# Weights of v in contiguous blocks, two loads cut in halves, and a new order for the first casts and products of an encoder layer

## The chip, the cores and the metric

The kernel runs on one core of one Trainium2 chip. The core has five engines that run their own instruction streams side by side: TensorE (PE, matrix products and transposes), VectorE (DVE), ScalarE (ACT), GpSimd (POOL) and SyncE (SP, which here only issues DMAs). TensorE reads SBUF and writes PSUM; DVE and ACT read PSUM, POOL does not. DMAs move data between HBM and SBUF. The metric is the device time of one execution in microseconds; smaller is better. Results are compared as the median of several runs.

## The reference

One layer of a bidirectional encoder on 1024 tokens of width 1024, in float32. The parts that matter here are the first ones: a LayerNorm of the input, and the products of its result with the columns of `w_in` that make q and v.

```python
def layer_norm(x, g, b):
    mu = jnp.mean(x, axis=-1, keepdims=True)
    var = jnp.mean(jnp.square(x - mu), axis=-1, keepdims=True)
    return (x - mu) * lax.rsqrt(var + LN_EPS) * g + b

h = layer_norm(x, emb_ln_g, emb_ln_b)                  # 1024 x 1024
proj = h @ w_in                                        # 1024 x 5120
q, k, v, z_a, u, z_b, g_a, g_b = jnp.split(proj, offs, axis=-1)
attn = neighbourhood_attention(q, k, v, rpb)           # 8 heads of 64
y_a = attn * silu(z_a)
h_lru = rg_lru(conv(u), forward) + rg_lru(conv(u), backward)
y_b = h_lru * silu(z_b)
m = sigmoid(g_a + b_merge[0]) * (y_a @ w_ba) + sigmoid(g_b + b_merge[1]) * (y_b @ w_bb)
out = layer_norm(ALPHA * h + m @ w_out, ln_g, ln_b)
```

## The kernel before

Tokens are handled in eight tiles of 128 (`x0` to `x7`), the width in eight blocks `k` of 128. Every float32 product is made of three products in a rounded format: an operand is split into a high part (a cast on ACT, names ending in `_hi`) and a low part (the difference between the value and its high part, names ending in `_lo`, on DVE or POOL). With activations `h` and weights `w` the three products are high times high, low times high and high times low. In `v_part(i, kind, ks)` (line 320) they are called `"h"` (high of h, high of w), `"a"` (low of h, high of w) and `"w"` (high of h, low of w); a tile of v takes 24 of them, eight blocks by three kinds, all added up in one PSUM bank.

The order of work is written out by hand for all engines: an engine runs its instructions in the order in which the program text issues them, and an instruction waits until its operands are there. An instruction that waits holds up everything behind it on its engine. On PE the order of the text is the order of the products. SP issues almost all loads and stores, in the order of the text too.

The stage that the change touches is the beginning, up to the first products of q, and it goes like this:

- Loads (lines 399 to 410): gains and biases of the LayerNorm, `x0` in two halves of 512 columns, v's weights in four loads of two blocks each (`load_wv`, line 191), `x1` between the second and the third, then `x2`, the first block of q's weights (`qk_load(0)`), `x3`, `x4` and some small tables. v's weights stand in HBM as 128 rows of 8 x 512 values, so that one load takes 4 KB out of each row of 16 KB.
- `warm_up(n)` (line 200) issues n small products of zeros on PE whose result is not used.
- `gb_spread` spreads the LayerNorm's gains and biases over all partitions, into four PSUM banks `gps`; `gb_copy(z, c)` (line 213, ACT) copies one of them to SBUF, where POOL can read it.
- The LayerNorm of a tile: `ln_stats` (DVE), `ln_root` (ACT), and then for tiles 0, 1 and 3 `ln_v(i, c)` (line 240, DVE, from the banks `gps`, one call per half of the columns), for the other tiles `ln_scale` (line 248, ACT) and `ln_g` (line 255, four operations on POOL, which need the copies of `gb_copy`; the first two make the left half, the last two the right one).
- `turn(i, kk)` (line 266): four transposes on PE of half a tile into one PSUM bank; `turn_hi` (line 278, ACT) and `turn_lo` (line 281, DVE) split the result into the blocks that the products read.
- `wv_hi(k)` (line 194, ACT) and `wv_lo(k)` (line 197, POOL) split block k of v's weights. `qk_prep(m)` (line 177) does the same for a block m of q's weights: `qk_hi` on ACT (line 171) and `qk_lo` on POOL. Only one raw block of q's weights fits at a time, so `qk_load(1)` can be issued when `qk_lo(0)` has read the first.
- `keep(i)` (line 261) stores a finished tile to HBM. `load_x(5)` goes into the place of `x0` and waits until `keep(0)` has landed.
- PE's own order in this stage: transposes of tile 0, 20 of the 24 products of v's tile 0, transposes of tile 1 with the rest of tile 0 and the products of tile 1 between them, 24 products of q (`q_part(0, 0)`, line 345, its matrix instructions stand in line 134), then 16 transposes: left half of tile 2, left half of tile 3, right half of tile 2, right half of tile 3 (`turned_in`, lines 512 to 518), then the products of v's tile 2.

PSUM banks of this stage come from a pool of four, in an order that the list `places` (line 86) writes out.

Of the kernel before, what the change touches and what calls it, by code (L numbers as in the profile page):

```python
# [15 lines left out]
P = 128  # L16
S = 1024
D = 1024
NK = D // P
# [4 lines left out]
HALF = 512  # L24
# [7 lines left out]
WARM = 18, 4, 6  # L32
# [35 lines left out]
def encoder_kernel(ctx, tc, x, gb1, gb, w_qk, w_v, w_s, w_ba, w_bb, w_gate, smalls, bias, w_out, out):  # L68
    nc = tc.nc
    V, A, G, PE, SP = nc.vector, nc.scalar, nc.gpsimd, nc.tensor, nc.sync  # L70
# [12 lines left out]
    hb12 = pool("hb12", "right")  # L83

    turns = []
    places = itertools.chain((0, 1, 2, 3, 0, 1, 2, 0, 2, 3, 1), itertools.cycle((2, 3, 0, 1)))

    def bank(name):
        if turns:
            return banks[0].tile([P, HALF], F32, tag=next(turns[0]), bufs=2, name=name)  # L90
        if banks[0] is ps0:
            return ps0.tile([P, HALF], F32, tag=f"b{next(places)}", bufs=1, name=name)
        return banks[0].tile([P, HALF], F32, tag="bank", name=name)
# [33 lines left out]
    def lo_of(eng, lo, full, hi):  # L127
        eng.tensor_tensor(lo, full, hi.bitcast(F32), ALU.subtract)  # L128
# [27 lines left out]
    wvs = [hts[0].tile([P, 4, HALF], F32, tag="ht4" + c, name=f"wvs{c}") for c in "hl"]  # L156
# [12 lines left out]
    def qk_hi(m):  # L169
        qk_w[m] = pair(wpl, [P, NK, P], f"wqk{m}", tag="w", bufs=2)  # L170
        A.copy(qk_w[m][0][:], qk_s[m][:])

    def qk_lo(m):
        hi, lo = qk_w[m]
        lo_of(G, lo[:], qk_s.pop(m)[:], hi[:])

    def qk_prep(m):
        qk_hi(m)
        qk_lo(m)
# [2 lines left out]

    def load_x(i):
        xs[i] = ln.tile([P, D], F32, tag="x", bufs=5, name=f"x{i}")
        if i == 0:
            for sl in halves:
                SP.dma_start(xs[i][:, sl], x[i][:, sl])
        else:
            SP.dma_start(xs[i][:], x[i])

    def load_wv(c):
        SP.dma_start(wvs[c // 2][:, 2 * (c % 2):2 * (c % 2) + 2, :], w_v[:, 2 * c:2 * c + 2, :])

    def wv_hi(k):
        A.copy(wv[0][k][:], wvs[k // 4][:, k % 4, :])

    def wv_lo(k):
        lo_of(G, wv[1][k][:], wvs[k // 4][:, k % 4, :], wv[0][k][:])

    def warm_up(n):  # L200
        for _ in range(n):
            PE.matmul(clock[:, :P], zero[:], zero[:], start=True, stop=True)
# [10 lines left out]
    def gb_copy(z, c):  # L213
        A.copy(gb_t[z][c][:], gps[z][c][:])

    def ln_stats(i):
        st, mv, e = (ln.tile([P, n], F32, tag=f"ln{n}{c}", bufs=2, name=f"ln{i}{c}")
                     for n, c in ((12, "t"), (2, "m"), (4, "e")))
        sts[i] = st, mv, e[:, 3:4], e[:, 0:3]
        sd, ve = sts[i][2:]  # L220
        for c in range(2):
            V.bn_stats(st[:, 6 * c:6 * c + 6], xs[i][:, halves[c]])
        V.bn_aggr(mv[:], st[:].rearrange("p (c s) -> p c s", c=2))
        V.tensor_scalar(ve[:, 0:1], mv[:, 1:2], EPS, -0.5, ALU.add, ALU.mult)

    def ln_root(i):
        st, mv, sd, ve = sts[i]
        A.activation(sd, mv[:, 1:2], AF.Sqrt, bias=eps_t[:])

    def ln_sums(i):  # L230
        ln_stats(i)
        ln_root(i)

    def ln_rstd(i):
        st, mv, sd, ve = sts[i]
        V.reciprocal(sd, sd)
        V.tensor_scalar(ve[:, 1:2], sd, sd, ve[:, 0:1], ALU.mult, ALU.mult)
        V.tensor_scalar(sd, ve[:, 1:2], 1.5, sd, ALU.add, ALU.mult)

    def ln_v(i, c):  # L240

        z, (st, mv, sd, ve), sl = xs[i], sts[i], halves[c]
        V.scalar_tensor_tensor(z[:, sl], z[:, sl], mv[:, 0:1], gps[0][c][:], ALU.subtract, ALU.mult)
        if c == 0:
            ln_rstd(i)
        V.scalar_tensor_tensor(z[:, sl], z[:, sl], sd, gps[1][c][:], ALU.mult, ALU.add)

    def ln_scale(i):

        z, (st, mv, sd, ve) = xs[i], sts[i]  # L250
        ln_rstd(i)
        V.tensor_scalar(ve[:, 2:3], mv[:, 0:1], -1.0, sd, ALU.mult, ALU.mult)
        A.activation(z[:], z[:], AF.Identity, bias=ve[:, 2:3], scale=sd)

    def ln_g(i):
        z = xs[i]
        for c in range(2):
            for w, op in enumerate((ALU.mult, ALU.add)):
                G.tensor_tensor(z[:, halves[c]], z[:, halves[c]], gb_t[w][c][:], op)
# [6 lines left out]
    def turn(i, kk):  # L266
        tp = tps[i, kk] = bank(f"tp{i}_{kk}")
        for k4 in range(4):
            k = 4 * kk + k4
            PE.transpose(tp[:, k4 * P:(k4 + 1) * P], xs[i][:, k * P:(k + 1) * P], ident[:])  # L270

    def ti(i):
        return slice((i % 4) * P, (i % 4 + 1) * P)

    def tp4(i, kk):
        return tps[i, kk][:].rearrange("p (k t) -> p k t", k=4)

    def turn_hi(i, kk):
        A.copy(blocks[kk][i // 4][0][:, :, ti(i)], tp4(i, kk))  # L279

    def turn_lo(i, kk):
        hi, lo = blocks[kk][i // 4]
        lo_of(V, lo[:, :, ti(i)], tp4(i, kk), hi[:, :, ti(i)])
# [36 lines left out]
    def v_part(i, kind, ks):  # L320

        if i not in vos:
            vos[i], vn[i] = bank(f"v{i}"), 0
        for k in ks:
            a = blocks[k // 4][i // 4][kind == "a"][:, k % 4, ti(i)]
            PE.matmul(vos[i][:], a, wv[kind == "w"][k][:], start=vn[i] == 0, stop=vn[i] == 23)  # L326
            vn[i] += 1
# [3 lines left out]
    def v_hi(i):  # L331
        vs = outs["v", i] = ln.tile([P, H, 2, DH], F32R, tag="vs", bufs=2, name=f"vs{i}")
        A.copy(vs[:, :, 0, :], vos[i][:].rearrange("p (h d) -> p h d", d=DH))
# [63 lines left out]
    K0, K1, KS, BOTH = range(4), range(4, 8), range(8), range(2)  # L397

    A.dma_start(gb_row[:], gb1.rearrange("o z (r f) -> (o z r) f", f=P))
    load_x(0)  # L400
    load_wv(0)
    load_wv(1)
    load_x(1)
    load_wv(2)
    load_wv(3)
    load_x(2)
    qk_load(0)
    load_x(3)
# [8 lines left out]
        gb_spread(z, c)  # L417
    warm_up(WARM[2])
    ln_sums(0)
    ln_v(0, 0)  # L420
    turn(0, 0)
    warm_up(WARM[2])
    wv_hi(0)
    wv_hi(1)
    turn_hi(0, 0)
    ln_v(0, 1)
    keep(0)
    load_x(5)
    turn(0, 1)
    warm_up(WARM[2])  # L430
    wv_hi(2)
    wv_hi(3)
    turn_hi(0, 1)
    turn_lo(0, 0)
    gb_copy(0, 0)
    wv_hi(4)
    wv_hi(5)
    ln_sums(1)
    turn_lo(0, 1)
    wv_hi(6)  # L440
    wv_hi(7)
    gb_copy(1, 0)
    for k in KS:
        wv_lo(k)
    qk_prep(0)
    for k in K0:
        v_part(0, "h", (k,))
        v_part(0, "a", (k,))
    v_part(0, "w", (0, 1))
    v_part(0, "h", (4, 5))  # L450
    v_part(0, "w", (2, 3))
    v_part(0, "h", (6, 7))
    v_part(0, "a", K1)
    ln_v(1, 0)
    ln_v(1, 1)
    keep(1)
# [1 line left out]
    load_x(6)  # L458
    turn(1, 0)
    turn_hi(1, 0)  # L460
    v_part(0, "w", (4, 5))
    v_part(1, "h", K0)
    turn(1, 1)
    for z in BOTH:
        gb_copy(z, 1)
    turn_hi(1, 1)
    v_part(0, "w", (6, 7))
    ln_stats(2)
    turn_lo(1, 0)
    ln_root(2)  # L470
    v_hi(0)
    ln_scale(2)
    turn_lo(1, 1)
    ln_g(2)
    v_part(1, "w", K0)
    v_part(1, "h", K1)
    v_part(1, "a", KS)
    v_part(1, "w", K1)
    ln_sums(3)
# [562 lines left out]
    for slot in range(7 * N_PAIR + 4):  # L1042
        p, k = divmod(slot, 7)
# [184 lines left out]
    for unit in range(-NT, H * NT + PV_LAG):  # L1228
        h, c = divmod(unit, NT)
# [381 lines left out]
    for slot in range(16 + len(plan)):  # L1611
# [28 lines left out]
        a, b, p = plan[slot - 16]  # L1640
# [11 lines left out]
    p, x, w = 3, banksX[3], banksW[3]  # L1652
# [11 lines left out]
    for n, part in pieces[2:] + pieces[:2]:  # L1664
        z = zs[p, 1, n]
# [89 lines left out]
```

## Time and profile before

| | |
|---|---|
| median of 3 runs | 665.61 us (665.5 to 665.76) |
| the profiled execution | 665.38 us, of which 663.6 us from first to last instruction |
| TensorE clock granted, mean | 0.995 |
| busy: PE / DVE / ACT / POOL | 98% / 79% / 59% / 60% of the span |
| DMA moved | 113.42 MB, mean 171 GB/s |

Times in the profile are microseconds from the start of the span. "Busy" counts what an engine's instructions take; on PE instructions overlap, and the end of a product is modelled. A row of the timeline has a start, a length, the engine, the line of the kernel, the operation, the tiles (written and read) and how many instructions were merged into it; in brackets behind it stands how long the engine was idle before it and what ended that. "SPq" is SP issuing a DMA: the length is that of the issue, not of the transfer.

### The profile page before, as it was taken

Reading aid. Unit: us, or ns where it says so; the run is one execution under the profiler, and the core shown is the slowest. Engines: PE = TensorE matmul, PEld = TensorE weight load, DVE = VectorE, ACT = ScalarE, POOL = GpSimd, SP = SyncE. Lnnn points to the kernel's source line nnn. Section 1 sums busy time; section 2 is a strip of 40 time slices with the busy share of each in tenths; the row PEclk is TensorE's granted clock in tenths of the full one; section 3 lists DMA queues with packets and bytes.
Section 4 is the critical chain, followed back from the end, with each engine's and each line's share of the span. In section 5 each row is a group of like instructions: output and inputs, shape, how many; then the busy total and the mean of one; then the engine's idle time right before and its main releaser. Section 6 shows DMA issues by size and latency. Waiting matters only on the chain.

```text
span 663.6 us, 9466 instructions
## 1 busy us (share of the span) xinstructions
PE 651.8 (98%) x3129; PEld 544.4 (82%) x3129; DVE 521.3 (79%) x860; ACT 388.2 (59%) x685; POOL 395.5 (60%) x315
## 2 busy tenths in 40 slices
PE   8999999999999999999999999999999999999994
PEld 7888888888888888888788888888888888888883
DVE  7978867786899599879987697277777876994776
ACT  5555433256786677777666834277777744574242
POOL 5898263434676476658556455012653549989857
PEclk9999999999999999999999999999999999999997
DMA  8746617033334133532361548898976288333023
GB/s 323 250 160 223 213 41 245 26 112 126 117 113 140 60 112 108 179 104 88 129 221 60 190 164 282 305 335 258 360 287 235 65 304 290 113 119 127 21 108 127
DMA packets 52193, 113.42 MB, mean 171 GB/s; under 512 B 5472, under 2 KB 9904, under 8 KB 50608
## 3 DMA queue, kind: packets, MB, share of 16 engines
q1 hardware_dynamic: 51680, 112.28, 49.0%
q8 instruction: 25, 0.41, 0.3%
q10 hardware_dynamic: 464, 0.53, 0.2%
q14 instruction: 24, 0.20, 0.1%
HBM read 77.11 MB, written 35.68 MB: 170 GB/s over the span
## 4 chain that ended last, share of the span: by engine, by line
PE 90%; DVE 5%; DMA 1%; issue 1%; SPq 1%; POOL 1%; ACT 0%; POOLq 0%; DVEq 0%; ACTq 0%
PE a L134 32%; PE mb L134 13%; PE s L134 12%; PE x L134 6%; PE v L326 6%; PE w L134 5%; PE acc L1147 4%; PE q L134 3%; PE s L1101 3%; PE pt L1123 3%; PE g L794 2%; DMA wqk_s<-in_w_qk_dram 1%; DVE ws_l L128 1%; PE tp L270 1%; DVE uc L752 1%
## 5 line engine op out<-in xcount | busy, mean ns | idle before, releaser
L134 PE MATMUL a<-ht_h,ws_h 128*128 128x512 f32 x136 | 53.1, 391 | 0.0
L134 PE MATMUL a<-ht_h,ws_l 128*128 128x512 f32 x136 | 53.0, 390 | 0.0
L134 PE MATMUL a<-b_h,wa_l 128*128 128x512 f32 x136 | 53.0, 389 | 0.0
L134 PE MATMUL a<-ht_l,ws_h 128*128 128x512 f32 x136 | 53.0, 389 | 0.0
L134 PE MATMUL a<-b_h,wa_h 128*128 128x512 f32 x136 | 52.9, 389 | 0.0
L134 PE MATMUL a<-b_l,wa_h 128*128 128x512 f32 x136 | 52.9, 389 | 0.0
L1111 DVE CUSTOM_DVE_ANT_0 sc<-s,bias 128x384 f32<-128x384 f32 (+1 forms) x64 | 33.4, 523 | 21.5 <-PE s L1101 14.1
L1131 ACT CAST pt_h<-pt 128x384 fp32r<-128x384 f32 x64 | 29.0, 453 | 25.3 <-PE pt L1123 17.3
L1116 ACT ACTIVATE p<-sc,summ 128x384 f32<-128x384 f32 (+1 forms) x64 | 37.9, 592 | 5.3 <-DVE summ L1111 5.1
L134 PE MATMUL mb<-ya,wb_h 128*128 128x512 f32 x128 | 39.6, 389 | 0.0
L902 POOL CAST wb_h<-wb 128x512 fp32r<-128x512 f32 x9 | 7.0, 777 | 47.6 <-DMA wb<-in_w_bb_dram 47.6
L128 DVE TENSOR_TENSOR pt_l<-pt,pt_h 128x384 fp32r<-128x384 f32 x64 | 33.2, 519 | 2.1 <-ACT pt_h L1131 1.6
L128 POOL TENSOR_TENSOR ht_l<-t,ht_h 128x512 fp32r<-128x512 f32 x16 | 22.0, 1410 | 19.9 <-ACT ht_h L312 19.9
L326 PE MATMUL v<-wv,b_h 128*128 128x512 f32 x128 | 32.9, 399 | 0.5 <-ACT b_h L279 0.5
L1513 POOL TENSOR_TENSOR z<-z,gb 128x512 f32<-128x512 f32 (+2 forms) x23 | 27.6, 1215 | 8.6 <-ACT z L1508 7.7
L1101 PE MATMUL s<-ks,qs 128*128 128x384 f32 (+1 forms) x128 | 31.3, 326 | 0.0
L134 PEld LDWEIGHTS a<-ht_h,ws_h 128*128 128x128 f32 x136 | 25.5, 188 | 6.0 <-issue 0.5
L1123 PEld LDWEIGHTS pt<-ident,p 128*128 128x128 f32 x176 | 23.1, 140 | 8.5
L134 PEld LDWEIGHTS a<-b_h,wa_h 128*128 128x128 f32 x136 | 25.5, 188 | 5.4
L134 PEld LDWEIGHTS a<-ht_l,ws_h 128*128 128x128 f32 x136 | 25.5, 188 | 5.4
L134 PEld LDWEIGHTS a<-b_h,wa_l 128*128 128x128 f32 x136 | 25.5, 188 | 5.3
L134 PEld LDWEIGHTS a<-b_l,wa_h 128*128 128x128 f32 x136 | 25.5, 188 | 5.3
(545 smaller groups left out, 2259.9 us busy)
## 6 DMA issues: line engine op xcount, KB each, us to landing
ks<-k_d SPq DMA_DIRECT2D x8, 1024.0 KB, 8.3
h_d<-x SPq DMA_DIRECT2D x8, 512.0 KB, 4.6
v_d<-vs SPq DMA_DIRECT2D x8, 512.0 KB, 3.5
q_d<-q SPq DMA_DIRECT2D x8, 512.0 KB, 3.0
ga_d<-ga SPq DMA_DIRECT2D x16, 256.0 KB, 2.3
gb_d<-gb SPq DMA_DIRECT2D x16, 256.0 KB, 2.4
k_d<-k SPq DMA_DIRECT2D x8, 512.0 KB, 3.4
qs<-q_d SPq DMA_DIRECT2D x8, 512.0 KB, 5.8
```

The lines of the kernel that those rows point to most:

```text
L128: eng.tensor_tensor(lo, full, hi.bitcast(F32), ALU.subtract)
L134: PE.matmul(o, a, b, start=first and i == 0, stop=last and i == len(prods) - 1, skip_group_check=not (first and last))
L326: PE.matmul(vos[i][:], a, wv[kind == "w"][k][:], start=vn[i] == 0, stop=vn[i] == 23)
L794: PE.matmul(o[:, n, :], w[:, 2 * d + b, :], us[b][:, n * HALF:(n + 1) * HALF], start=z == 0, stop=z == 1)
L902: G.tensor_copy(hi[:], st[:])
L1101: PE.matmul(o[:, :P * len(near(t))], q[:, t * P:(t + 1) * P], k[:, z, keys], start=z == 0, stop=z == 1)
L1111: V.tensor_tensor_reduce(s[:, :w], o[:, :w], heads[h][2][:, b0:b0 + w], -1.0, 3.0e38, ALU.add, ALU.min, accum_out=sums[h][0][:, t:t + 1])
L1116: A.activation(probs[h % 2][t][:], scs.pop((h, t))[:, :w], AF.Exp, bias=sums[h][0][:, t:t + 1], scale=-1.0, accum_out=sums[h][1][:, t:t + 1])
L1123: PE.transpose(tp[:, n * P:(n + 1) * P], probs[h % 2][t][:, z * P:(z + 1) * P], ident[:])
L1131: A.copy(pt[0][:, span(b)], tps[h, b][:, :P * len(near(b))])
L1147: PE.matmul(acc[g][:, d:d + w], vvs[h // 2][:, b, h % 2, :], pt[:, a:a + w], start=b in (1, 6) and z == 0, stop=z == 1 and b == (4, 7)[g])
L1513: G.tensor_tensor(z, z, gbs[c, n][:, part], (ALU.mult, ALU.add)[c])
```

## The change

Four things change, all in the beginning of the kernel.

1. v's weights stand in HBM in four blocks, one per load, each contiguous (4 x 128 x 2 x 512 values). The first of the four loads is issued as two, one block of 128 x 512 values each; `x1` is issued as two halves like `x0`. That makes two more DMAs on SP's queue.
2. The order on ACT: the cast of the first weight block goes ahead of the first `turn_hi`; the casts of blocks 1 to 3 come behind it in one run; the copies of gains and biases (`gb_copy`) move from between the weight casts to behind `ln_root(2)`; the split of q's first weight block (`qk_prep(0)`, ACT and POOL) moves from before v's products to behind `turn_hi(1, 0)`; `v_hi(0)` moves back.
3. The order on PE: one product of v's tile 0 (block 0, `"h"`) goes ahead of the transposes of the right half of tile 0, and the six `warm_up` products behind those transposes go away. The `"w"` products of tile 0 are spread among the others one by one, and the last four of them and those of tile 1 change places with the products around them. The number of products is the same.
4. The list of PSUM banks follows: v's tile 0 now takes the bank that the right half of tile 0 took, and the other way round, and so on for the tiles behind them.

```diff
-    places = itertools.chain((0, 1, 2, 3, 0, 1, 2, 0, 2, 3, 1), itertools.cycle((2, 3, 0, 1)))
+    places = itertools.chain((0, 1, 2, 3, 0, 1, 3, 0, 3, 2, 1, 3, 2, 0, 1), itertools.cycle((2, 3, 0, 1)))
...
     def load_x(i):
         xs[i] = ln.tile([P, D], F32, tag="x", bufs=5, name=f"x{i}")
-        if i == 0:
+        if i < 2:
             for sl in halves:
                 SP.dma_start(xs[i][:, sl], x[i][:, sl])
...
     def load_wv(c):
-        SP.dma_start(wvs[c // 2][:, 2 * (c % 2):2 * (c % 2) + 2, :], w_v[:, 2 * c:2 * c + 2, :])
+        for part in ((0,), (1,)) if c == 0 else ((0, 1),):
+            k = 2 * (c % 2) + part[0]
+            SP.dma_start(wvs[c // 2][:, k:k + len(part), :], w_v[c][:, part[0]:part[-1] + 1])
...
     ln_sums(0)
+    wv_hi(0)
     ln_v(0, 0)
     turn(0, 0)
+    turn_hi(0, 0)
     warm_up(WARM[2])
-    wv_hi(0)
-    wv_hi(1)
-    turn_hi(0, 0)
+    v_part(0, "h", (0,))
     ln_v(0, 1)
     keep(0)
     load_x(5)
     turn(0, 1)
-    warm_up(WARM[2])
-    wv_hi(2)
-    wv_hi(3)
+    for k in (1, 2, 3):
+        wv_hi(k)
     turn_hi(0, 1)
     turn_lo(0, 0)
-    gb_copy(0, 0)
     wv_hi(4)
     wv_hi(5)
     ln_sums(1)
     turn_lo(0, 1)
     wv_hi(6)
     wv_hi(7)
-    gb_copy(1, 0)
     for k in KS:
         wv_lo(k)
-    qk_prep(0)
-    for k in K0:
+    v_part(0, "h", (1,))
+    v_part(0, "a", (0, 1))
+    v_part(0, "h", (2,))
+    v_part(0, "a", (2,))
+    v_part(0, "w", (0,))
+    v_part(0, "h", (3,))
+    v_part(0, "a", (3,))
+    v_part(0, "w", (1,))
+    v_part(0, "h", (4, 5))
+    v_part(0, "w", (2,))
+    v_part(0, "a", (4, 5))
+    for k in (6, 7):
         v_part(0, "h", (k,))
         v_part(0, "a", (k,))
-    v_part(0, "w", (0, 1))
-    v_part(0, "h", (4, 5))
-    v_part(0, "w", (2, 3))
-    v_part(0, "h", (6, 7))
-    v_part(0, "a", K1)
+    v_part(0, "w", (3,))
     ln_v(1, 0)
     ln_v(1, 1)
     keep(1)
     qk_load(1)
     load_x(6)
     turn(1, 0)
     turn_hi(1, 0)
-    v_part(0, "w", (4, 5))
+    qk_prep(0)
+    v_part(0, "w", (4,))
     v_part(1, "h", K0)
     turn(1, 1)
-    for z in BOTH:
-        gb_copy(z, 1)
     turn_hi(1, 1)
-    v_part(0, "w", (6, 7))
+    v_part(0, "w", (5, 6))
     ln_stats(2)
     turn_lo(1, 0)
     ln_root(2)
-    v_hi(0)
+    for z in BOTH:
+        gb_copy(z, 0)
+    v_part(1, "w", K0)
     ln_scale(2)
+    for z in BOTH:
+        gb_copy(z, 1)
     turn_lo(1, 1)
     ln_g(2)
-    v_part(1, "w", K0)
     v_part(1, "h", K1)
+    v_part(0, "w", (7,))
+    v_hi(0)
     v_part(1, "a", KS)
     v_part(1, "w", K1)
...
-        "w_v": w_in[:, 1024:1536].reshape(NK, P, HALF).transpose(1, 0, 2),
+        "w_v": w_in[:, 1024:1536].reshape(4, 2, P, HALF).transpose(0, 2, 1, 3),
```

## The prediction, made before the changed kernel ran

> **What bounds the kernel now.** I read the page first, then the busy time by windows, the waits, the chain of the first 60 us in order of time, and last the timelines of PE, ACT, POOL, DVE and SP over the first 40 us. The page and the windows (columns: length of the stretch, then busy time and count of PE, then clock, DMA share and GB/s at the end):
>
> ```profile
> span 663.6 us, 9466 instructions
> PE 651.8 (98%) x3129; PEld 544.4 (82%) x3129; DVE 521.3 (79%) x860; ACT 388.2 (59%) x685; POOL 395.5 (60%) x315
> ...
> 9.91:23.38 13.47, 12.98 (x61) 9.61 (x59) 11.63 (x30) 9.53 (x18) 12.41 (x10) 1.00 0.82 302
> 23.38:28.00 4.62, 4.62 (x42) 4.62 (x41) 4.45 (x10) 2.49 (x5) 4.27 (x4) 1.00 0.76 290
> 120.00:300.00 180.00, 180.00 (x791) 147.81 (x790) 152.59 (x163) 122.16 (x152) 104.99 (x76) 1.00 0.33 110
> ```
>
> PE is busy 98% of the span; it has gaps up to 23.38, none from there to 28, and none from 120 to 300. So the changed stage, PE's first 28 us, passes what it wins or loses to the end one for one, if nothing takes it back on the way; and it can win only what PE idles or repeats there. PE in this stage, with the row of its weight loads (PEld) that waits:
>
> ```profile
> 9.11 0.66 PE L270 MATMUL tp<-ident,x 128*128 128x128 f32 x4 [0.23 <-DVE x L246]
> 9.61 0.50 PE L202 MATMUL clock<-zero 128*128 128x128 bf16 x6
> 9.91 0.48 PE L326 MATMUL v<-wv,b_h 128*128 128x512 f32 x1
> ...
> 16.86 1.20 PE L326 MATMUL v<-wv,b_h 128*128 128x512 f32 x4 [0.47 <-ACT b_h L279]
> 17.89 0.60 PE L270 MATMUL tp<-ident,x 128*128 128x128 f32 x4
> 23.38 0.28 PE L134 MATMUL q<-b_h,wqk_h 128*128 128x256 f32 x1
> 26.25 1.91 PE L270 MATMUL tp<-ident,x 128*128 128x128 f32 x16
> 27.91 3.94 PE L326 MATMUL v<-wv,b_h 128*128 128x512 f32 x16
> 28.83 0.76 PEld L326 LDWEIGHTS v<-wv,b_h 128*128 128x128 f32 x4 [0.19 <-ACT b_h L279]
> 31.69 1.98 PE L326 MATMUL v<-wv,b_l 128*128 128x512 f32 x8
> 33.50 3.79 PE L326 MATMUL v<-wv,b_h 128*128 128x512 f32 x16
> 37.13 1.03 PE L270 MATMUL tp<-ident,x 128*128 128x128 f32 x8
> ```
>
> Prices: 16 products of v without a wait take 37.13 - 33.50 = 3.63, that is 0.227 each; four transposes (26.25 + 4 x 0.415 = 27.91) take 0.415; the 24 products of q take 26.25 - 23.38 = 2.87. From 9.91 to 23.38 PE does 48 products of v (10.90) and 8 transposes (0.83), 11.73 of 13.47 us: 1.74 us are gaps. The 16 products at 27.91 took 31.69 - 27.91 = 3.78 in place of 3.63: 0.15 us lost where the second four waited for ACT at 28.83. Those 1.9 us are all there is to win.
>
> **POOL and ACT are the hidden bounds.** Their rows:
>
> ```profile
> 7.60 1.14 ACT L195 CAST wv<-wvsh 128x512 fp32r<-128x512 f32 x2 [2.05 <-DMA wvsh<-in_w_v_dram]
> 8.64 0.58 ACT L279 CAST b_h<-tp 128x512 fp32r<-128x512 f32 x1
> 9.12 1.14 ACT L195 CAST wv<-wvsh 128x512 fp32r<-128x512 f32 x2
> 11.45 1.14 ACT L195 CAST wv<-wvsl 128x512 fp32r<-128x512 f32 x2 [0.21 <-DMA wvsl<-in_w_v_dram]
> 15.27 1.05 ACT L171 CAST wqk_h<-wqk_s 128x1024 fp32r<-128x1024 f32 x1 [0.92 <-DMA wqk_s<-in_w_qk_dram]
> 18.53 0.59 ACT L279 CAST b_h<-tp 128x512 fp32r<-128x512 f32 x1 [0.75 <-PE tp L270]
> 20.35 1.25 ACT L253 ACTIVATE x<-x,ln2e 128x1024 f32<-128x1024 f32 x1 [0.56 <-DVE ln2e L252]
> 26.09 1.05 ACT L171 CAST wqk_h<-wqk_s 128x1024 fp32r<-128x1024 f32 x1 [1.93 <-DMA wqk_s<-in_w_qk_dram]
> ...
> 8.30 5.04 POOL L128 TENSOR_TENSOR wv<-wvsh,wv 128x512 fp32r<-128x512 f32 x4 [6.99 <-ACT wv L195]
> 13.30 5.02 POOL L128 TENSOR_TENSOR wv<-wvsl,wv 128x512 fp32r<-128x512 f32 x4
> 18.28 2.42 POOL L128 TENSOR_TENSOR wqk_l<-wqk_s,wqk_h 128x1024 fp32r<-128x1024 f32 x1
> 21.67 5.28 POOL L259 TENSOR_TENSOR x<-x,gb 128x512 f32<-128x512 f32 x4 [0.98 <-ACT x L253]
> ...
> 14.38 0.75 DVE L246 SCALAR_TENSOR_TENSOR x<-x,ln1e,gps 128x512 f32<-128x512 f32 x1 [0.62 <-ACT gb L214]
> ```
>
> POOL works from 8.30 to 20.70 without a pause, then on tile 2's LayerNorm until 21.67 + 5.28 = 26.95. The transposes of tile 2's right half start at 26.25 + 2 x 0.415 = 27.08: 0.13 us of slack. And ACT waits for the second block of q's weights until 26.09; behind that cast stand tile 2's and 3's high parts, and the second four products of v at 28.83 need one of them: no slack at all. SP's queue tells when that block is asked for:
>
> ```profile
> 10.22 0.33 SPq L262 DMA_DIRECT2D h_d<-x  x1
> 19.28 0.33 SPq L189 DMA_DIRECT2D x<-in_x_dram  x1
> 19.70 0.38 SPq L262 DMA_DIRECT2D h_d<-x  x1
> 20.72 0.33 SPq L167 DMA_DIRECT2D wqk_s<-in_w_qk_dram  x1
> ...
> SPq L189 <- DMA h_d<-x: 12.4, 2, 8.7
> x<-in_x_dram SPq DMA_DIRECT2D x1, 512.0 KB, 4.2
> x<-in_x_dram SPq DMA_DIRECT2D x1, 512.0 KB, 3.0
> ```
>
> The load of x5 waits 8.7 us for tile 0's store, which stands behind all the first loads; behind it on the same queue go tile 1's store and then q's second weights. The last two rows are the loads issued at 19.28 and at 24.82, with their us to landing.
>
> **The change part by part.** *First cast early.* The first weight block is now cast on ACT before the first high part (8.64). It must land by then; it lands by 7.60 today, and is half as large now. POOL's first split thus leaves the chain, but its second one waits for the cast behind the high part: 8.64 + 0.48 (the pitch to 9.12) = 9.12, + 0.62 of one cast (1.14 for two at a pitch of 0.52) + 0.08 (as 7.60 + 0.62 to 8.30) = 9.82. Seven splits at (5.04 + 5.02)/8 = 1.257 end at 18.62, against 18.32. The split of q's weights ends at 21.0 against 20.70. Then tile 2 follows at once, if its scaling on ACT is done: before it ended at 20.35 + 1.25 = 21.60, so this must come 0.6 earlier (below). POOL ends tile 2 at 21.0 + 5.3 = 26.3 in place of 26.95.
>
> *PE's order.* The product moved ahead waits for the first high part (8.64 + 0.58 = 9.22), and the right half's transposes behind it on PE go from 9.11 to 9.45. That costs nothing: their high part follows three casts on ACT, 9.12 + 3 x 0.52 = 10.7, when their result has been there since 9.45 + 0.66 = 10.1. The six idle products that go (0.3 us of PE until 9.91) were filler; the granted clock in the windows is 1.00, and the longest gap below is 0.6 against 0.47 today. Walking on at 0.227 a product: blocks 0 to 3 run through to 12.0; blocks 4 and 5 wait for their casts (11.45 at the landing of today, done 12.6), 6 and 7 for a load that by the rate below lands 1.35 later (12.8, cast by 13.9), with three products behind the last cast: the 20 products end at 14.6.
>
> *Copies moved.* DVE waited 0.62 at 14.38 for a copy of gains by ACT out of the bank that it reads; that copy is gone from there. Tile 1's left half is ready at 14.38 - 0.62 + 0.75 = 14.51, its transposes run at 14.6. Of the four copies two now stand ahead of the scaling of tile 2 on ACT, at most 1.14 for the two (as two casts of that shape), two behind it.
>
> *q's weights moved.* Today ACT waits 0.92 for them until 15.27 and casts 1.05 before tile 1's first high part, for which PE then waits 0.47. Now the high part comes first: 14.6 + 0.64 (17.89 to 18.53, transposes to cast) + 0.58 = 15.8, with PE waiting from 15.25, one product after the transposes. The cast of q's weights lies behind it, done by 16.9, while tile 1's second high part comes at 17.4. Four products to 16.7, transposes to 17.15, then 23 products with all operands there: 22.4, or 22.5 with small change, so q's products begin 0.9 earlier than 23.38. Their low weights are ready at 21.0. Tile 2's scaling: the second high part ends at 18.0; from its end to the scaling it is 1.23 today (18.53 + 0.59 to 20.35), the two copies lie beside the DVE work in it and may stretch it to 1.5: start 19.5, end 20.75, before the 21.0 that POOL needs. DVE's low parts behind that, today done just ahead of their products, move with it.
>
> *Sum.* q's products end at 22.5 + 2.87 = 25.4, the first eight transposes at 26.2, and then PE waits for POOL until 26.3: against 27.08 the gain is 0.78, and the 0.15 lost at 28.83 falls away if ACT is in time. The ties above (blocks 4 to 7, DVE's low parts, 21.0 against 20.75) can take back 0.1 to 0.3. I take 0.8.
>
> *The layout and the halves* decide whether ACT is in time. No row shows a contiguous weight load, so bounds: x0's halves land at 3.40 and 4.28 (DVE's first rows), and 512 KB at 389 GB/s, the rate of the next windows, are 1.35 us:
>
> ```profile
> 3.40 0.69 DVE L222 BATCH_NORM_STATS2 ln0t<-x 128x6 f32<-128x512 f32 x1 [2.40 <-DMA x<-in_x_dram]
> 4.28 0.69 DVE L222 BATCH_NORM_STATS2 ln0t<-x 128x6 f32<-128x512 f32 x1 [0.19 <-DMA x<-in_x_dram]
> 8.00:10.00 2.00, 1.77 (x23) 1.57 (x22) 1.65 (x3) 2.00 (x5) 1.70 (x2) 1.00 1.03 389
> ```
>
> So the first weights could be there at 5.6, and came at 7.60: 2.0 late, and all loads behind them with it. At the pace of x0's halves (0.88 each) they come at 6.04, 1.56 earlier. The other end: x5, contiguous, needed 4.2 us, so a contiguous load can stumble too, and halves at 0.88 against 0.67 cost 0.2 each, for four halves: from 0.8 late to 2.0 early. I take 1.5 early, for x0's halves are the nearest rows in place, size and layout. Then x0's store lands and x5 starts that much earlier, and q's second weights come at the later of 26.09 - 1.5 = 24.6 and 21.0 + 3.0 to 4.2 = 24.0 to 25.2. ACT's chain from there to the second four products is 28.83 - 26.09 = 2.74, so they can run at 27.9 or earlier; PE brings them at 26.3 + 0.83 + 0.91 = 28.04. In time.
>
> [...]
>
> **The rivals.** *The loads come no earlier.* q's second weights land at 26.09 as today, the second four products stay at 28.83, and all that PE won before goes into that wait: 0 to 0.1 gained, 665.5. For it speaks that x5 stumbled in contiguous rows; against it, x0's halves. *All gaps go.* If POOL's and ACT's chains come out shorter than their rows, PE's 1.74 go, 663.9; against it stands POOL's chain of twelve operations, none of which the change shortens. *Slower: q's second weights land later than today.* The halves add two DMAs and smaller pieces ahead of x0's store; if the stumble of 2.0 us comes twice, x5 and all behind it shift, and PE waits at the second four products of v's tile 2, one for one: 2.0 later is 667.6. It decides from 1.33 on, a landing after 27.4. Against it: steady loads follow one another evenly in the rows at hand.
>
> **How the numbers follow.** The profiled execution took 665.38, 663.6 of it span; minus 0.8 it is 664.6. The median of the runs is 0.23 higher, so 664.8. What a measurement can tell from no change is about 0.2%, 1.33 us. Chances: the forecast 0.47, loads no earlier 0.17, all gaps gone 0.20, slower 0.16. The forecast and the first rival end within 0.2%, but for 0.07 of the forecast above 1.33 and 0.02 of the first rival below: faster 0.27, same 0.55, slower 0.18. The range reaches from the all-gaps case to somewhat beyond a lost race for q's weights: 663.7 to 666.1, leaving out most of the slow case. The forecast's own range is 664.5 to 665.1.
>
> **What would show it.** Right: POOL's second weight split starts near 9.8 and the chain runs without a pause into tile 2, ending near 26.3; ACT's cast of q's second weights starts before 25.3; PE's q products begin near 22.5 and its transposes wait for POOL near 26.2; DVE's 0.62 wait is gone. Wrong: a first weight block after 8.6, which moves ACT's first high part and POOL's chain; tile 2's scaling ending after 21.0; q's second weights after 25.3.

## The result, and the profile after

| | before | changed |
|---|---|---|
| median of 20 runs each | 665.82 us (665.15 to 667.18) | 664.98 us (664.4 to 666.03) |
| the profiled execution | 665.38 us, span 663.6 | 664.93 us, span 663.1 |

The ratio is 0.9986 with an interval of 0.998 to 0.9992: the change gains 0.84 us in the median. The interval leaves out 1, so the gain is clear of noise in this comparison, but it is less than the 1.33 us that the prediction counted as a difference. The two profiled executions lie only 0.45 us apart; before's was one of its quicker ones (665.38 against a median of 665.82).

The page of the changed kernel, and busy time by windows (length, busy time and count of PE first; clock, DMA share and GB/s last):

```profile
span 663.1 us, 9459 instructions
PE 651.1 (98%) x3123; PEld 544.0 (82%) x3123; DVE 523.9 (79%) x860; ACT 388.2 (59%) x685; POOL 396.7 (60%) x315
...
22.35:27.00 4.65, 4.65 (x41) 4.52 (x39) 4.48 (x10) 2.03 (x4) 3.90 (x4) 1.00 0.86 325
120.00:300.00 180.00, 180.00 (x791) 147.84 (x790) 155.12 (x168) 122.17 (x152) 105.57 (x75) 1.00 0.33 111
```

Nothing moved in the long part: PE has no gap from 120 to 300, before as after. The clock is 1.00 too. All that happened is in the first 33 us. The timeline of PE (start, length, engine, line, operation, tiles, count, idle time before it):

```profile
9.05 0.50 PE L328 MATMUL v<-wv,b_h 128*128 128x512 f32 x1 [0.34 <-ACT b_h L281]
9.39 0.60 PE L272 MATMUL tp<-ident,x 128*128 128x128 f32 x4
...
14.36 0.60 PE L272 MATMUL tp<-ident,x 128*128 128x128 f32 x4
15.64 1.20 PE L328 MATMUL v<-wv,b_h 128*128 128x512 f32 x4 [0.42 <-ACT b_h L281]
...
22.35 0.28 PE L134 MATMUL q<-b_h,wqk_h 128*128 128x256 f32 x1
...
25.23 1.93 PE L272 MATMUL tp<-ident,x 128*128 128x128 f32 x16
27.14 4.18 PE L328 MATMUL v<-wv,b_h 128*128 128x512 f32 x16
31.15 1.98 PE L328 MATMUL v<-wv,b_l 128*128 128x512 f32 x8
32.97 3.79 PE L328 MATMUL v<-wv,b_h 128*128 128x512 f32 x16
```

Before, the products of q began at 23.38, those of v's tile 2 at 27.91, those of v's tile 3 at 33.50. Now these are 22.35, 27.14 and 32.97: a lead of 1.03 us shrinks to 0.77 and then to 0.53. The first loss: 16 transposes take 27.91 - 26.25 = 1.66 without a wait, so they end at 25.23 + 1.66 = 26.89, and PE begins v's tile 2 only at 27.14 (0.25 lost). The second: the 16 products behind take 31.15 - 27.14 = 4.01, against 31.69 - 27.91 = 3.78 before. Directly behind the transposes they took 3.75, not 3.63, where ACT made nobody wait (shown below), so 0.26 us are lost here and 0.03 were lost before. The timelines of ACT, POOL, DVE and SP say who held it up:

```profile
5.72 0.62 ACT L197 CAST wv<-wvsh 128x512 fp32r<-128x512 f32 x1
...
15.00 0.58 ACT L281 CAST b_h<-tp 128x512 fp32r<-128x512 f32 x1 [1.59 <-PE tp L272]
15.48 1.05 ACT L171 CAST wqk_h<-wqk_s 128x1024 fp32r<-128x1024 f32 x1
25.55 1.05 ACT L171 CAST wqk_h<-wqk_s 128x1024 fp32r<-128x1024 f32 x1 [2.41 <-DMA wqk_s<-in_w_qk_dram]
26.51 1.06 ACT L281 CAST b_h<-tp 128x512 fp32r<-128x512 f32 x2
...
6.42 1.26 POOL L128 TENSOR_TENSOR wv<-wvsh,wv 128x512 fp32r<-128x512 f32 x1 [5.11 <-ACT wv L197]
9.59 3.82 POOL L128 TENSOR_TENSOR wv<-wvsh,wv 128x512 fp32r<-128x512 f32 x3 [1.91 <-ACT wv L197]
20.73 5.28 POOL L261 TENSOR_TENSOR x<-x,gb 128x512 f32<-128x512 f32 x4
...
13.32 0.75 DVE L248 SCALAR_TENSOR_TENSOR x<-x,ln1e,gps 128x512 f32<-128x512 f32 x1
...
18.74 0.33 SPq L189 DMA_DIRECT2D x<-in_x_dram  x1
19.16 0.39 SPq L264 DMA_DIRECT2D h_d<-x  x1
20.79 0.33 SPq L167 DMA_DIRECT2D wqk_s<-in_w_qk_dram  x1
```

ACT waits for q's second weights until 25.55, casts them, and only then makes the high parts of tiles 2 and 3 (26.51; the first is done at 26.51 + 0.58 = 27.09, and PE starts at 27.14). POOL's tile 2 ends at 20.73 + 5.28 = 26.01, and PE reaches it at 25.23 + 2 x 0.415 = 26.06: POOL holds up nothing. What is left of the limit is the load of q's second weights. It goes last of three transfers of 512 KB: x5 (issued at 18.74) landed 4.2 us after its issue, at 22.9; tile 1's store (19.16) 5.1 us after, at 24.3; and q's weights were there by 25.55.

### The profile page after: what moved, and what is told of

It is laid out like the page before. It is cut to its first block, busy times and chain, and to the rows that moved or that the text cites. A ratio compares the mean times of both kernels' runs of the same rounds, so it can differ in the third digit from the quotient of the medians.

```text
span 663.1 us, 9459 instructions
## 1 busy us (share of the span) xinstructions
PE 651.1 (98%) x3123; PEld 544.0 (82%) x3123; DVE 523.9 (79%) x860; ACT 388.2 (59%) x685; POOL 396.7 (60%) x315
## 4 chain that ended last, share of the span: by engine, by line
PE 92%; DVE 5%; issue 1%; POOL 1%; DMA 0%; ACT 0%; POOLq 0%; SPq 0%; DVEq 0%; ACTq 0%
PE a L134 32%; PE mb L134 13%; PE s L134 12%; PE v L328 7%; PE x L134 6%; PE w L134 5%; PE acc L1156 4%; PE q L134 3%; PE s L1110 3%; PE pt L1132 3%; PE g L803 2%; PE tp L272 1%; DVE ws_l L128 1%; DVE uc L761 1%; DVE wa_l L128 1%
## 5 line engine op out<-in xcount | busy, mean ns | idle before, releaser
L1120 DVE CUSTOM_DVE_ANT_0 sc<-s,bias 128x384 f32<-128x384 f32 (+1 forms) x64 | 33.5, 523 | 21.7 <-PE s L1110 14.2
L1140 ACT CAST pt_h<-pt 128x384 fp32r<-128x384 f32 x64 | 29.0, 453 | 25.3 <-PE pt L1132 17.2
```

What stands on the lines that cost most here:

```text
L1120: V.tensor_tensor_reduce(s[:, :w], o[:, :w], heads[h][2][:, b0:b0 + w], -1.0, 3.0e38, ALU.add, ALU.min, accum_out=sums[h][0][:, t:t + 1])
L1140: A.copy(pt[0][:, span(b)], tps[h, b][:, :P * len(near(b))])
```

## The experiments

The theory: v's tile 3 begins at the later of two chains. One is PE's own, from the start of q's products on. The other is ACT's, from the landing of q's second weights, and it ends last in the changed kernel. The rivals: POOL still sets the end; the row pitch, not the halves, moves the loads; the new order alone brings the gain.

T3 stands for the start of v's products of tile 3. All readings in one table, each from the profiled execution (us from the start of the span): the issue of x5's load, ACT's cast of q's second weights, the start of q's products, T3, the span less T3, and the times with their ratio to before. The ratios are to the runs of before measured beside each kernel (medians 665.79 to 666.18 for the kernels below "changed"), so they are not the quotients of the medians shown.

| kernel | x5 issued | q's second cast | q begins | T3 | span - T3 | median | ratio (interval) |
|---|---|---|---|---|---|---|---|
| before | 19.28 | 26.09 | 23.38 | 33.50 | 630.1 | 665.82 | 1 |
| changed | 18.74 | 25.55 | 22.35 | 32.97 | 630.1 | 664.98 | 0.9986 (0.998 to 0.9992) |
| loads only, one run | 19.58 | 26.28 | 23.76 | 33.88 | 630.4 | 666.05 | |
| loads only, timed | 18.57 | 25.22 | 22.71 | 32.82 | 630.1 | 665.06 | 0.9989 (0.998 to 0.9998) |
| order only | 20.20 | 26.92 | 23.86 | 34.33 | 630.1 | 665.72 | 0.9996 (0.9988 to 1.0005) |
| whole blocks, one run | 19.57 | 26.09 | 23.25 | 33.50 | 630.1 | 665.42 | |
| whole blocks, timed | 19.27 | 25.94 | 22.91 | 33.37 | 630.5 | 665.74 | 0.9998 (0.9989 to 1.0007) |
| halves, old pitch | 19.05 | 25.85 | 22.55 | 33.24 | 630.1 | 665.43 | 0.9993 (0.9984 to 1.0002) |
| q's weights ahead of x5 | 21.12 | 23.93 | 22.46 | 32.56 | 630.1 | 664.20 | 0.9977 (0.9968 to 0.9986) |
| the same, q's split back | 21.21 | 24.39 | 22.82 | 32.95 | 630.2 | 665.41 | 0.999 (0.9982 to 0.9999) |
| the same, copies back | 21.07 | 24.14 | 23.07 | 33.18 | 630.1 | 665.22 | 0.9992 (0.9983 to 1.0001) |
| the same, two products later | 21.07 | 24.06 | 22.17 | 32.31 | 630.1 | 664.30 | 0.9977 (0.9968 to 0.9986) |
| q's weights behind x6, one run | 20.03 | 31.14 | 23.63 | 39.92 | 630.0 | 671.69 | |

Three things can be read from it. From T3 to the end every kernel takes 630.0 to 630.5 us, so what differs is decided by T3. In all rows but the last, T3 is the later of "q begins + 10.11" and "q's second cast + 7.41", within 0.04 us; both constants were read off these rows, so this describes them and is no independent test. PE's constant does come out of its rows where ACT makes nobody wait (q's weights ahead of x5): 2.87 for q's products, 1.67 for the transposes, 3.75 for 16 products and 1.81 for the next 8 make 10.10. And as long as x5, and no other late load, goes ahead of q's second weights on SP's queue (tile 1's store is between them each time), their cast comes 6.5 to 6.8 us after x5's issue.

**One part alone: the loads.** Before's order with the new layout and the halves:

```diff
-        if i == 0:
+        if i < 2:
...
-        SP.dma_start(wvs[c // 2][:, 2 * (c % 2):2 * (c % 2) + 2, :], w_v[:, 2 * c:2 * c + 2, :])
+        for part in ((0,), (1,)) if c == 0 else ((0, 1),):
+            k = 2 * (c % 2) + part[0]
+            SP.dma_start(wvs[c // 2][:, k:k + len(part), :], w_v[c][:, part[0]:part[-1] + 1])
```

> The order of before with the new layout and the halves alone. Theory A (ACT's wait for q's second weight block sets when v's tile 2 goes on): tile 0's store lands about 0.5 us earlier, q's second weights are cast from about 25.5 in place of 26.09, q's first ones before 15.0, and the products of v's tile 3 start near 33.0 (33.50 before, 32.97 in the changed kernel); one run near 664.9. Theory B (PE's new order and the moved copies make the gain, the loads are hidden): products of v's tile 3 stay at 33.4 to 33.5, no gain.

One execution, 666.05 us, where 664.9 was expected. The loads of x5 and q's second weights came later than in before, in spite of the halves, and so did q's first weights (cast at 15.67; before, 15.27). By the table it is the first weights that count here: T3 is q's start + 10.11, and ACT's chain (26.28 + 7.41 = 33.69) ends ahead of it (the timelines of SP and ACT):

```profile
19.58 0.33 SPq L189 DMA_DIRECT2D x<-in_x_dram  x1
15.67 1.05 ACT L171 CAST wqk_h<-wqk_s 128x1024 fp32r<-128x1024 f32 x1 [0.93 <-DMA wqk_s<-in_w_qk_dram]
26.28 1.05 ACT L171 CAST wqk_h<-wqk_s 128x1024 fp32r<-128x1024 f32 x1 [1.74 <-DMA wqk_s<-in_w_qk_dram]
```

So the same kernel was timed with more runs.

> The order of before with layout and halves, timed. In one profile the first half landed at 5.8 and the second at 7.9, tile 0's store no earlier than before, and q's second weights were cast at 26.28. If that is the rule, the loads alone are worth nothing: 0.9995 to 1.0008. If the loads come 0.5 earlier on the mean, ACT's two waits for q's weights shrink by it: 0.9988 to 0.9995.

```profile
18.57 0.33 SPq L189 DMA_DIRECT2D x<-in_x_dram  x1
14.62 1.05 ACT L171 CAST wqk_h<-wqk_s 128x1024 fp32r<-128x1024 f32 x1 [0.94 <-DMA wqk_s<-in_w_qk_dram]
```

0.9989: the loads alone bring nearly what the whole change brings. T3 is q's start + 10.11 here too, and in the old order q begins 8.09 to 8.11 us after the cast of q's first weights in all three profiles (15.27 and 23.38 before, 15.67 and 23.76, 14.62 and 22.71). In before both chains end together (33.49 and 33.50). So theory A had nearly the right T3 (33.0 expected, 32.82 measured), but the wait that sets it here is another: in the old order the loads go with PE's start of q by way of q's first weights, which the new order takes out of that path. The two parts of the change thus work in part on the same wait, and their gains need not add. The same store lands, and lets x5 go, at 19.58 in one execution of this kernel and at 18.57 in another: that scatter is larger than the effect looked for.

**The other part alone: the order.** The changed kernel with before's layout and whole loads:

```diff
-        if i < 2:
+        if i == 0:
...
-        for part in ((0,), (1,)) if c == 0 else ((0, 1),):
-            k = 2 * (c % 2) + part[0]
-            SP.dma_start(wvs[c // 2][:, k:k + len(part), :], w_v[c][:, part[0]:part[-1] + 1])
+        SP.dma_start(wvs[c // 2][:, 2 * (c % 2):2 * (c % 2) + 2, :], w_v[:, 2 * c:2 * c + 2, :])
```

> The changed order with the loads of before (rows 16 KB apart, no halves beside x0's). Theory A: q's products start near 22.5, but q's second weights are cast at about 26.1 as before, the wait on PE at v's tile 2 grows to about 1 us, and the products of v's tile 3 start at 33.4 to 33.5: ratio to before 0.9995 to 1.0005. Theory B: the products of v's tile 3 start at 33.0 or earlier, ratio 0.9986 to 0.9992.

665.72 us, 0.9996: no difference that can be told. The profiled execution, at 666.16, is one of the longest of the eleven. In it the first weights came late (8.63, with 2.48 us of ACT idle), and all behind them: q's start at 23.86 (22.5 expected), x5 at 20.20, q's second cast at 26.92, T3 at 34.33 (33.4 to 33.5 expected).

```profile
8.63 0.62 ACT L195 CAST wv<-wvsh 128x512 fp32r<-128x512 f32 x1 [2.48 <-DMA wvsh<-in_w_v_dram]
26.92 1.05 ACT L171 CAST wqk_h<-wqk_s 128x1024 fp32r<-128x1024 f32 x1 [2.28 <-DMA wqk_s<-in_w_qk_dram]
```

**The disputed wait taken away: q's second weights ahead of x5.** The changed kernel, with one load moved on SP's queue:

```diff
     keep(0)
-    load_x(5)
...
     qk_load(1)
+    load_x(5)
     load_x(6)
```

> The changed kernel with q's second weight block issued ahead of x5 on SP's queue (x5 follows it). Theory A: issued at 20.8, it lands between 23.8 and 25.0, ACT no longer makes PE wait at v's tile 2, and the products of v's tile 3 start at 32.3 to 32.5 in place of 32.97; 0.4 to 0.65 us faster than the changed kernel, ratio to before about 0.998. Theory B: nothing moves, 32.9 to 33.0.

664.20 us (664.07 to 664.8), 0.9977. The timelines of SP, ACT and PE:

```profile
9.82 5.92 SPq L264 DMA_DIRECT2D h_d<-x  x2
20.68 0.33 SPq L167 DMA_DIRECT2D wqk_s<-in_w_qk_dram  x1
21.12 0.85 SPq L189 DMA_DIRECT2D x<-in_x_dram  x2
23.93 1.05 ACT L171 CAST wqk_h<-wqk_s 128x1024 fp32r<-128x1024 f32 x1 [0.68 <-DMA wqk_s<-in_w_qk_dram]
25.97 1.07 ACT L281 CAST b_h<-tp 128x512 fp32r<-128x512 f32 x2 [0.99 <-PE tp L272]
27.00 3.92 PE L328 MATMUL v<-wv,b_h 128*128 128x512 f32 x16
30.75 1.98 PE L328 MATMUL v<-wv,b_l 128*128 128x512 f32 x8
32.56 3.79 PE L328 MATMUL v<-wv,b_h 128*128 128x512 f32 x16
```

The load is issued when it was (20.68 against 20.79), but is there 3.25 us later, not 4.76 (20.79 to 25.55). So its issue was not what made it late, but what stood ahead of it. That is more than x5: the first row merges the stores of tiles 0 and 1, and tile 1's store, which in the changed kernel stood on SP's queue behind x5's wait and went at 19.16, goes at 15.42 here. The edit takes both x5's 512 KB and that store's 512 KB out of the way, and no run parts the two in this order. With the cast at 23.93, ACT now waits for PE's transposes, as it should, and T3 is PE's own chain (22.46 + 10.11), 0.41 earlier than in the changed kernel (32.56; 32.3 to 32.5 expected). The theory holds: T3 moved when the second weights came earlier, with q's start 0.11 later than in the changed kernel. The 16 products behind the transposes take 30.75 - 27.00 = 3.75 with no wait for ACT: this is what they cost at that place.

**The wait made longer: q's second weights behind x6.** The changed kernel with two loads changing places:

```diff
-    qk_load(1)
     load_x(6)
+    qk_load(1)
```

> The changed kernel with q's second weight block issued behind x6, which waits for tile 1's store. If ACT's wait for this block sets the pace of PE, the cast moves from 25.55 to about 28.2 and the products of v's tile 3 from 32.97 to about 35.6, one for one, and the time by about 2.6 us, to 667.5. If PE has other work to cover it, the products of v's tile 3 stay below 34.

```profile
31.14 1.04 ACT L171 CAST wqk_h<-wqk_s 128x1024 fp32r<-128x1024 f32 x1 [6.73 <-DMA wqk_s<-in_w_qk_dram]
32.73 5.54 PE L328 MATMUL v<-wv,b_h 128*128 128x512 f32 x16 [4.31 <-ACT b_h L281]
38.10 1.99 PE L328 MATMUL v<-wv,b_l 128*128 128x512 f32 x8
...
33.00:36.00 3.00, 3.00 (x8) 2.35 (x8) 2.51 (x7) 2.56 (x5) 1.92 (x2) 0.50 0.31 111
```

671.69 us in one execution, far more than the 667.5 expected; the last row is a window of 3 us, with the granted clock third from the end. The cast comes 5.59 later than in the changed kernel (2.65 were expected; x5 alone was issued 1.29 later here), T3 6.95 later and the span is 6.8 longer. The direction is that of the slow rival, and the loss reaches the end in full, but not one for one: 1.36 us come on top, in the 16 products, which take 38.10 - 32.73 = 5.37 against 4.01 in the changed kernel. The granted clock accounts for it: behind PE's gap of 4.31 us it stands at 0.98 from 32 to 33, 0.50 from 33 to 36 and 0.82 from 36 to 37, then at 1.00 again. By an estimate from these windows 0.02 + 3 x 0.50 + 0.18 = 1.70 us of clock are lost, and the products take 5.37 - 3.75 = 1.62 longer than without a wait. In the changed kernel the clock is 1.00 from 8 to 36. This run also has a load without a store ahead of q's weights: x6's, issued 0.42 us before them. They are cast 5.16 us after their issue, against 3.25 above, so a load alone delays them too.

**The halves or the layout?** The changed kernel without the halves, contiguous blocks kept:

```diff
-        if i < 2:
+        if i == 0:
...
-        for part in ((0,), (1,)) if c == 0 else ((0, 1),):
-            k = 2 * (c % 2) + part[0]
-            SP.dma_start(wvs[c // 2][:, k:k + len(part), :], w_v[c][:, part[0]:part[-1] + 1])
+        SP.dma_start(wvs[c // 2][:, 2 * (c % 2):2 * (c % 2) + 2, :], w_v[c])
```

> The changed kernel with contiguous blocks, but without the halves of the first weight load and of x1 (two DMAs fewer). If the layout brings the loads forward, the first weights land near 5.8 to 6.0, all later loads as early as in the changed kernel or up to 0.3 earlier, and the products of v's tile 3 start at 32.7 to 33.0. If the halves do it, the first weights land near 7.5 as before and the products start near 33.4.

One execution, 665.42 us; then timed:

> The changed kernel with contiguous blocks and no halves beside x0's, timed. In one profile the first weights landed at 7.98, as late as in rows 16 KB apart, and nothing was won. If the halves bring the loads forward, the ratio to before is 0.9992 to 1.0003, as with the changed order alone (0.9996). If the layout does and that profile was a stray, 0.9982 to 0.999, as in the changed kernel.

665.74 us, 0.9998. And the halves without the layout:

```diff
-            SP.dma_start(wvs[c // 2][:, k:k + len(part), :], w_v[c][:, part[0]:part[-1] + 1])
+            j = 2 * c + part[0]
+            SP.dma_start(wvs[c // 2][:, k:k + len(part), :], w_v[:, j:j + len(part), :])
```

> The changed kernel with the halves, but v's weights in rows 16 KB apart as before. If the halves bring the loads forward, the first weight block is cast from 5.8 to 6.2, tile 0's store lands near 18.7 and the ratio to before is 0.9982 to 0.999. If the layout does, the first weights land after 7, q's second weights are cast at 26 or later and the ratio is 0.9992 to 1.0003.

665.43 us, 0.9993. Its expectation named this ratio for the layout, but the first cast came as it said for the halves (5.62), and q's second cast, at 25.85, just ahead of the 26 named for the layout. POOL's first row of whole blocks, timed, and then of halves at the old pitch:

```profile
8.37 5.20 POOL L128 TENSOR_TENSOR wv<-wvsh,wv 128x512 fp32r<-128x512 f32 x4 [7.06 <-ACT wv L195]
```

```profile
6.30 1.27 POOL L128 TENSOR_TENSOR wv<-wvsh,wv 128x512 fp32r<-128x512 f32 x1 [4.99 <-ACT wv L198]
```

The halves are what brings the first weight block early: POOL's first split starts at 8.30 to 9.34 in the four profiles with whole loads and at 6.30 to 7.39 in the nine with halves, at either pitch and in either order. The Trainium skill (DMA: Bandwidth & Descriptors, Latency and other measured facts) lists row pitches from 512 KiB up, for copies between HBM tensors: 207 GB/s at 512 KiB, where 214 is the full rate, and 164 at 2 MiB. It has no figure for 16 KB; here that pitch shows no cost at the first split (6.30 at the old pitch, 6.42 contiguous). The same page (Bandwidth) asks for DMAs of 1 MiB or more; here cutting 512 KB in two did the first consumer good. In the total time neither half of the edit is told apart: the intervals of 0.9998, 0.9993 and 0.9986 overlap, so what each is worth alone stays open.

But the halves do not make the stream faster. What the DMAs had moved in the first 8 us and in the next 10, before and then changed:

```profile
DMA packets 683, 1.89 MB, mean 237 GB/s; under 512 B 79, under 2 KB 95, under 8 KB 683
...
DMA packets 1205, 3.88 MB, mean 388 GB/s; under 512 B 269, under 2 KB 269, under 8 KB 1204
```

```profile
DMA packets 902, 1.86 MB, mean 233 GB/s; under 512 B 108, under 2 KB 124, under 8 KB 902
...
DMA packets 1287, 3.96 MB, mean 396 GB/s; under 512 B 273, under 2 KB 273, under 8 KB 1286
```

By 8 us the changed kernel has moved no more (1.86 MB against 1.89), by 18 us 0.05 MB more. That fits a first block that is there earlier because it is a smaller piece; x0's store and x5, which come behind all the loads, gain little.

**Undoing one step of the order, with q's weights freed.** Since the order shows nothing while the load hides it, its steps were undone in the kernel with q's weights ahead of x5. First `qk_prep(0)` back before v's products:

```diff
     for k in KS:
         wv_lo(k)
+    qk_prep(0)
...
     turn_hi(1, 0)
-    qk_prep(0)
```

> The kernel with q's second weights ahead of x5, and the split of q's first weight block back where it was, ahead of tile 1's first high part. Theory: these weights land near 14.9, ACT casts them until 15.9 and the high part comes at 15.85 in place of 15.08; PE's wait before tile 1's products grows from 0.44 to about 1.2, q's products start near 23.2 in place of 22.46, and 0.75 us of the gain go: ratio to before 0.9985 to 0.9992. If the move was hidden anyway, 0.9977 as with that kernel.

```profile
14.52 1.05 ACT L171 CAST wqk_h<-wqk_s 128x1024 fp32r<-128x1024 f32 x1 [1.22 <-DMA wqk_s<-in_w_qk_dram]
16.10 1.20 PE L328 MATMUL v<-wv,b_h 128*128 128x512 f32 x4 [0.89 <-ACT b_h L281]
22.82 0.28 PE L134 MATMUL q<-b_h,wqk_h 128*128 128x256 f32 x1
```

PE's wait for tile 1's high part doubles (0.89 against 0.44), and q begins 0.36 later; less than the 0.75 expected, for q's first weights came at 14.52 here, where 14.9 was expected (15.27 in before). The wait is shown; the 0.36 is not, for q begins at 22.35 to 23.63 in the four profiles of the new order with halves that leave this step in and the copies where they are (changed, old pitch, q's weights ahead of x5, behind x6). In time it is 0.999 against 0.9977, intervals overlapping. Then the four copies back in their old places:

```diff
     turn_lo(0, 0)
+    gb_copy(0, 0)
...
     wv_hi(7)
+    gb_copy(1, 0)
...
-    for z in BOTH:
-        gb_copy(z, 0)
...
     turn(1, 1)
+    for z in BOTH:
+        gb_copy(z, 1)
```

> The kernel with q's second weights ahead of x5, and the four copies of gains back between the weight casts. Theory: DVE waits 0.5 to 0.6 for the second copy before it ends tile 1's left half, the transposes of tile 1 run near 14.8 to 15.0 in place of 14.45, and 0.4 to 0.6 us of the gain go: ratio 0.9983 to 0.999. If DVE's wait is hidden behind PE's products, no more than 0.1 goes.

```profile
14.16 0.75 DVE L248 SCALAR_TENSOR_TENSOR x<-x,ln1e,gps 128x512 f32<-128x512 f32 x1 [0.79 <-ACT gb L216]
...
15.06 0.63 PE L272 MATMUL tp<-ident,x 128*128 128x128 f32 x4 [0.23 <-DVE x L248]
23.07 0.28 PE L134 MATMUL q<-b_h,wqk_h 128*128 128x256 f32 x1
```

DVE's wait for the copy is back (0.79), tile 1's transposes wait for DVE in turn (15.06 in place of 14.45), and q begins 0.61 later. In this one trace the wait lies on PE's path; its price in q's start is within the scatter named above. The time is 665.22 us, 0.9992 against 0.9977, intervals overlapping.

**A further step:** two of tile 0's products (block 7, `"a"`, and block 3, `"w"`) moved behind tile 1's first transposes, where PE waits 0.42 in the changed kernel (0.44 with q's weights ahead of x5, the kernel that this builds on).

```diff
+    v_part(0, "h", (6,))
+    v_part(0, "a", (6,))
+    v_part(0, "h", (7,))
...
     qk_prep(0)
+    v_part(0, "a", (7,))
+    v_part(0, "w", (3,))
```

> The kernel with q's second weights ahead of x5, and two of the products of v's tile 0 moved behind tile 1's left transposes, where PE waits 0.44 for their high part. The transposes move from 14.45 to about 14.1, when DVE has tile 1's left half, the wait falls to about 0.1, and q's products start near 22.15 in place of 22.46: 0.3 us faster, ratio about 0.9972. If DVE's half is what the transposes wait for, nothing is won.

```profile
14.15 0.63 PE L272 MATMUL tp<-ident,x 128*128 128x128 f32 x4
14.85 1.80 PE L328 MATMUL v<-wv,b_h 128*128 128x512 f32 x6
22.17 0.28 PE L134 MATMUL q<-b_h,wqk_h 128*128 128x256 f32 x1
```

The wait is gone and T3 is 0.25 earlier than without the step, but the ratio is 0.9977 in both: 0.25 us is below what these runs can show. These two kernels beat both before and the changed one by their medians (664.20 and 664.30 against 664.98; the intervals of their ratios, 0.9968 to 0.9986, and of the changed kernel's, 0.998 to 0.9992, overlap).

## Why the prediction was right, and where it was not

The forecast of 664.8 us and "no difference that counts" came out (664.98, a ratio inside 0.2% of 1). Its last step did not, and the number came out in part by luck. By its steps:

- **First cast early, POOL's chain: right.** POOL's second split started at 9.59 (9.82 forecast), and tile 2's LayerNorm followed without a pause at 20.73 and ended at 26.01 (26.3). The 0.3 it was early sufficed that PE does not wait for it at all; the forecast had put the new limit there.
- **PE's order: right.** The right half's transposes moved to 9.39 (9.45), and tile 1's began at 14.36 (14.6). Granted clock 1.00 without the six filler products.
- **Copies: right.** DVE's wait of 0.62 is gone from its row at 13.32; undone, it came back with 0.79, and q began 0.61 later in that one profile.
- **q's split: right in place.** Tile 1's high part comes at 15.00 (15.24), q's cast behind it at 15.48, and q's products begin at 22.35 (22.5).
- **The layout and the halves: the step that failed.** "I take 1.5 early ... In time." The first weight block did come early (cast at 5.72, assumed 6.04), but x0's store was issued only 0.46 earlier (9.76 against 10.22) and x5 only 0.54 (18.74 against 19.28), and q's second weights were cast 0.54 earlier too (25.55, not 24.6). That is past the 25.3 that the prediction named as its own sign of failure. The mechanism, a wait of the second four products for ACT, was the one described; the size of the lead was not. The step took the lead of the first block for a lead of the whole stream, while the bytes moved by 8 us were about the same (1.86 MB against 1.89). Its other bound failed as well: "21.0 + 3.0 to 4.2" was 20.79 + 4.76, for it priced the load without x5's load and tile 1's store ahead of it. With both out of the way it was 3.25.
- **The sum: 0.93 forecast before rounding down, 0.53 measured at T3.** Up to v's tile 2 both give 27.13 or 27.14, a gain of 0.77, but by different limits: the forecast had PE wait for POOL, the run shows it waiting 0.25 for ACT. What is missing is the last term: 0.15 was to fall away at the second four products, and the 16 products took 0.23 longer than before (4.01 against 3.78). The 0.15 was read wrongly from the start: 3.63 is what such products take elsewhere, at that place they take 3.75 without any wait for ACT, so only 0.03 could be won. The forecast's 0.8 then met a median 0.84 lower; the profiled pair itself differs by 0.45, so part of that closeness is luck.

The rivals: "The loads come no earlier" described what happens at that place better than the forecast did: the gain won before runs into ACT's wait. It was wrong in that the loads did come 0.54 earlier, and about that much is kept in the profiled pair. "Slower" needed a landing after 27.4; the latest in any kernel with before's queue order was 26.92, in the order alone. "All gaps go" was not reached by the change: PE still waits 0.42 for tile 1's high part and 0.25 at v's tile 2.

Open: whether the lead of the loads comes from the halves, the layout or the scatter between executions (x5's issue lies at 18.57 to 20.03 with halves, at 19.27 to 20.20 without), and how much of the wait for q's second weights is x5's load and how much tile 1's store.

## What to carry to other kernels

Cutting the first load in two brought its first consumer forward here, not the stream behind it: price what stands behind a full DMA queue by bytes and rate, stores included, and follow the load that the last waiting consumer needs (here a later one, behind x5's load and tile 1's store, 512 KB each). When two chains meet at a later point, work out both to that point and take the later; what is won in one is lost up to the end of the other. Issuing the load that is needed first ahead of one whose buffer merely came free first came with 0.41 us at T3 in the profiles and 0.78 us between the medians here (664.98 to 664.20), where the whole change had 0.53 and 0.84; the intervals of the two kernels overlap. A load that waits on an in-order queue also holds up what is issued behind it: here a store that went at 15.42 in place of 19.16 once that load was behind it.

## What the runs showed of the hardware that was not expected

- The first loads of the same kernel come at different times: x0's store landed, and x5 was issued, at 19.58 and 18.57 in two executions of the loads-only kernel, at 19.57 and 19.27 in two of the whole blocks. The scatter is there when the store is issued, not only when it lands: x5's issue follows the store's by 8.93 to 9.06 us in eight of the nine profiles in which x5 is ahead of q's second weights (9.42 at the old pitch), while the store's own issue lies at 9.55 to 11.26.
- Behind a gap of 4.31 us on PE the granted clock was 0.50 for 3 us (q's weights behind x6); behind the gaps of the changed kernel, 0.42 and less from 9 us on, it stayed at 1.00.
- Two of the kernels with q's second weights ahead of x5 scatter little: 664.07 to 664.8 and 664.05 to 664.55 in 11 runs each, against 664.4 to 666.03 in 20 runs of the changed kernel and 665.0 to 666.31 in 11 of the order alone. That fits a scatter of the loads that enters through that wait, but the two kernels with a step undone have the same queue order and scatter by 1.07 and 1.74 us, so it is not shown.
